# Block 1 of a two-block transformer kernel: modulation sums moved to the stage of keys and values, projections spread over all attention turns, convolution taps moved

## The chip, the cores and the metric

One core of a Trainium2 chip (trn2). The metric is the device time of one execution in microseconds (us), the median of several runs. Engines: PE multiplies matrices (PEld is its weight load), DVE is the vector engine, ACT the scalar engine, POOL GpSimd; SP's queue (SPq) issues the weight loads.

## The reference

Two transformer blocks over 512 tokens of width 1024. The first one, up to its mixture of experts, is what the change touches:

```
m = silu(c) @ w_mod + b_mod        # 6 x 1024 columns: shift, scale, gate, twice; also for the context rows
h, hc = modulate(rmsnorm(x), sh1, sc1), modulate(rmsnorm(ctx), sh1c, sc1c)
proj = h @ w_in                    # q, k, v (512 each), glu (1024), gate_att (1024), gate_conv (1024)
att = neighbourhood_attention(q, k, v, k_ctx, v_ctx, rpb)      # 8 heads; 512 local + 256 context keys
u = a * sigmoid(g)                 # a, g: the halves of glu
y = silu(layernorm(conv(u, conv_w) + conv_b))                  # depthwise, 31 taps, 512 channels
x = x + g1 * ((sigmoid(gate_att) * (att @ w_ao) + sigmoid(gate_conv) * (y @ w_co)) @ w_o)
```

After it come a mixture of 32 experts, a second attention block and an expert layer with product keys. None of that code changes.

## The kernel before, in words

`do_b1` runs four stages. Activations lie transposed: 1024 channels as 8 tiles of 128 partitions, 512 tokens in the free dimension. A float32 product is made of three matmuls (`mm3`, lines 327 to 329) of a high part H, cast by ACT (line 180), and a low part L = x - H, made by DVE or POOL (line 189). One output tile of 128 channels, a projection, is 8 x 3 matmuls.

**Loads.** `Loader` keeps a ring of five 1 MB tiles (`ringA`) and loads the units in the order in which `b1_plan` lists them; a unit leaves when the oldest has been freed (line 116, on SP's queue, which goes in order). Kinds: ("in", m) is a column tile m of w_in, two (or, for the values, two row halves) to a unit; ("m1", 0 to 7) are modulation units multiplied on PE (`mod_unit`); ("m1", 8 to 23) are rows of w_mod's transpose (`w_modr`), for which `mod_rows` makes two DVE instructions with a running sum (line 594, 128x1024 times the row `crow`, which is silu(c) spread over all partitions). `Splitter` makes H and L ahead of use, two pieces ahead in block 1.

**Stage 1, `project1`.** Norms, modulation of the latent and context rows, queries; then `keys`: four column tiles (m = 4 to 7) for latent and context rows (the cast of tile 5 stands on ACT behind the last copy of the queries, line 745), then `value_steps` over units 4 and 5. The activation Silu of `crow` stands in the values (lines 763 and 764, with a table load before and after).

**Stage 2, `attention1`.** 16 turns, four head pairs by four blocks of 128 queries. In a turn: the next turn's score products (line 862), its minimum on DVE (`least`, lines 875 to 880), this turn's transposes on PE (912) and copies on ACT (317), the next turn's exponents on ACT (888, 889), the product with the values (921, into a spare piece of the score tile), the copy of its result, and the next turn's scaling (896, 897 on DVE, 899 on ACT). Between these `Fill` puts PE's projections in steps of three matmuls: `fill1`, eight glu tiles over turns 0 to 7, one each; `fill2`, four tiles of gate_att over turns 8 to 15, half of one each. After each of the first eight turns stand `mod_rows` of one or two units (`early`). `glu_end` makes u for two channel tiles, with a table switch on ACT, when four glu tiles are there, and for the other two from turn 8. From then on `conv` puts convolution taps on DVE (`conv_steps`, line 782 the first of a channel tile, 786 the 30 others; the running sum is `g`, in SBUF): a credit of 2.4 ahead of the product with the values and of 2.4 behind the scaling, at 0.66 a tap.

**Stage 3, `merge`.** Twelve more gate projections (m = 4 to 15), with up to nine taps after each; at m = 12 the convolution is finished and PE's sums for the layernorm over it follow (line 241). Then the output products.

Of the kernel before, what the change touches and what calls it, by code (L numbers as in the profile page):

```python
# [285 lines left out]
class Kern:  # L286
# [231 lines left out]
                else:  # L518
                    sp.add_rows(key, 16 if s[0] == "d" else 2, 2, half)

    @staticmethod
    def early(n):

        return (2 * n, 2 * n + 1) if n < 5 else (n + 5,)

    def b1_plan(self):

        plan = [("m1", 0), ("m1", 4)] + [("in", m) for m in range(4)]
        for u in range(1, 4):
            plan += [("m1", u), ("m1", 4 + u)]  # L530
        plan += [("in", m) for m in range(4, 12)]
        self.fill1 = []
        for m, i in enumerate((0, 1, 4, 5, 2, 3, 6, 7)):
            self.fill1 += [("in", 12 + i)]
            plan += [("in", 12 + i)] + [("m1", 8 + j) for j in self.early(m)]
        plan += [("in", 20 + m) for m in range(16)]
        for n in ("ao", "co", "wo"):
            for m in range(8):
                plan.append((n, m))
                if n == "wo":  # L540
                    plan.append(("m2", m))
                elif n == "ao" and m in (1, 3, 5):
                    plan.append(("m1", 21 + m // 2))
        return plan
# [36 lines left out]
            nc.tensor.matmul(pm[:, h, :], sb[:, h * 128:(h + 1) * 128], self.c("msel"), start=True, stop=True)  # L581
        nc.scalar.copy(self.mod1[:, 2 * u:2 * u + 2, :], pm)

    def mod_row(self, pool, i):

        self.crow = pool.tile([128, D], F32, name="crow")
        self.nc.gpsimd.dma_start(out=self.crow, in_=self.ap["crow"][:, i * D:(i + 1) * D])

    def mod_rows(self, which, u):
# [52 lines left out]
    def do_b1(self):  # L642
        nc, tc, ap = self.nc, self.tc, self.ap
        V = nc.vector
        with ExitStack() as es:
            hp = es.enter_context(tc.tile_pool(name="h", bufs=1))
            sm = es.enter_context(tc.tile_pool(name="sm", bufs=1))
            self.sp.ahead = 2
            self.sp.low = "g"
            self.sp.use(es.enter_context(tc.tile_pool(name="w", bufs=1)))  # L650
            cv = es.enter_context(tc.tile_pool(name="cv", bufs=1))
            hH = hp.tile([128, KD, T], F32R, name="hH", tag="hH")
            hL = hp.tile([128, KD, T], F32R, name="hL", tag="hL")
            h = (hH, hL)
            x = self.xT
            self.mod_row(sm, 0)
            qT = cv.tile([128, 4, T], F32, name="qT", tag="qT")
            with ExitStack() as e2:
                kv = e2.enter_context(tc.tile_pool(name="kv", bufs=1))
                kT = kv.tile([128, 4, T + CTX], F32, name="kT")  # L660
                v = kv.tile([128, 6, 512], F32, name="v")
                with tc.tile_pool(name="ps1", bufs=1, space=PSUM) as ps, tc.tile_pool(name="w0", bufs=1) as w0:
                    self.mod_start(w0)
                    nc.scalar.preload_act_table_set("natural_log_exp_and_others")
                    self.project1(cv, w0, ps, sm, x, h, qT, kT, v)
                u_t = cv.tile([128, 4, T + 30], F32, name="u", tag="u")
                g_t = cv.tile([128, 4, T], F32, name="g", tag="g")
                gA = cv.tile([128, 4, T], F32, name="gA", tag="gA")
                nc.gpsimd.memset(u_t[:, :, 0:15], 0.0)
                nc.gpsimd.memset(u_t[:, :, 15 + T:], 0.0)  # L670
                conv = Fill([self.conv_steps(u_t, g_t)], 124 * 0.66)
                self.attention1(h, qT, kT, v, u_t, g_t, gA, conv, sm)
            self.merge(hp, cv, h, g_t, qT, gA, conv, sm)
        self.sp.ahead = 1
        self.sp.pool = None

    def project1(self, hcp, extra, ps, sm, x, h, qT, kT, v):
# [24 lines left out]
        for u in range(4):  # L702
# [3 lines left out]
                self.mod_unit("m1", 4 + u, ps, extra)  # L706
            if u == 0:
                nc.sync.dma_start(out=cx, in_=ap["ctx"])
            else:
                part(2 * u - 2, (2, 3))  # L710
            self.mod_flush(ps)
# [35 lines left out]
        def keys(w, m, lat):  # L747
            pt = ps.tile([128, T], F32, name="pt", tag="fl", bufs=4)[:, :T if lat else CTX]
            for k in range(KD):
                g = h if lat else hc  # L750
                self.mm3(pt, (w[0][:, k], w[1][:, k]), (g[0][:, k], g[1][:, k]), k == 0, k == KD - 1)
            nc.scalar.copy(kT[:, m - 4, 0 if lat else T:T if lat else T + CTX], pt)
        w = [self.sp.get(("in", 2)), self.sp.get(("in", 2), False)]
        for lat in (True, False):
            for i in range(2):
                keys(w[i], 4 + i, lat)
        for m in (6, 7):
            w = self.sp.get(("in", 3))
            for lat in (True, False):
                keys(w, m, lat)  # L760
        for n, _ in enumerate(self.value_steps(("in", 4), ps, h, v, hc, (("fl", 4, 1),))):
            if n == 2:
                nc.scalar.activation(self.crow, self.crow, AF.Silu)
                nc.scalar.preload_act_table_set("natural_log_exp_and_others")
            if n in (8, 30):
                self.load_bias((8, 30).index(n) * 2, 2)
        self.sp.low = "g"
# [9 lines left out]
    def conv_steps(self, u_t, y):  # L777
# [1 line left out]
        V = self.nc.vector  # L779
        cw = self.p("conv_w").rearrange("p (k t) -> p k t", k=4)  # L780
        for k in range(4):
            V.tensor_scalar(y[:, k], u_t[:, k, 0:T], cw[:, k, 0:1], self.p("conv_b")[:, k:k + 1],
                            op0=OP.mult, op1=OP.add)
            yield 0.66
            for t in range(1, 31):
                V.scalar_tensor_tensor(y[:, k], u_t[:, k, t:t + T], cw[:, k, t:t + 1], y[:, k],
                                       op0=OP.mult, op1=OP.add)
                yield 0.66

# [38 lines left out]
    def attention1(self, h, qT, kT, v, u_t, g_t, gA, conv, sm):  # L828
# [3 lines left out]
        with tc.tile_pool(name="a1", bufs=1) as a1, tc.tile_pool(name="ps2", bufs=1, space=PSUM) as ps:  # L832
# [16 lines left out]
            def gate(m):  # L849
                return self.dmaj_steps(("in", 10 + m // 2), h, ps, lambda pt: nc.scalar.copy(gA[:, m], pt))  # L850

            fill1 = Fill([glu(i - 12) for n, i in self.fill1], 8 * 5.3)
            fill2 = Fill([gate(m) for m in range(4)], 4 * 5.3)
            spare = [None]

            def products(hp, i):
# [73 lines left out]
            for n, (hp, i) in enumerate(seq):  # L930
# [5 lines left out]
                        self.load_bias(2 * seq[n + 1][0] + 4, 2)  # L936
                else:
                    spare[0] = ps.tile([128, CTX + 128], F32, name="cxs0", tag="cxs0")[:, CTX:]
                fill, left = (fill1, 8 - n) if n < 8 else (fill2, 16 - n)
                us = fill.left / left  # L940
                PTs = turn(Ps, fill)
                if nxt:
                    Ps = exps(cxs, Pm)
                fill.run(0.5 * us - 0.7)
                if n > first:
                    conv.run(2.4)
                if (n >= 8 or first > n) and len(glus) >= 4 * (1 + (n >= 8)) and ends:
                    first = min(first, n)
                    glu_end(ends.pop(0))
                pv(hp, i, PTs)  # L950
                if nxt:
                    scaled(Ps)
                fill.run(0.5 * us)
                if left == 1:
                    fill.finish()
                if n < 8:
                    for j in self.early(n):
                        self.mod_rows("m1", 8 + j)
                if n > first:
                    conv.run(2.4)  # L960

# [38 lines left out]
    def merge(self, hp, cv, h, y, att, gA4, conv, sm):  # L1000
        nc, tc, ap = self.nc, self.tc, self.ap
        V = nc.vector
        with tc.tile_pool(name="mg", bufs=1) as mg, tc.tile_pool(name="ps3", bufs=1, space=PSUM) as ps:
# [9 lines left out]
                nc.scalar.activation(gA4[:, m], gA4[:, m], AF.Sigmoid)  # L1013
            na = 0
            norm = self.layernorm(cv, ps, sm, y)
            for m in range(4, 16):
                i = 20 + m
                g = gA(m) if m < 8 else gB[:, m - 8]
# [1555 lines left out]
```

## Time and profile before

| | us |
|---|---|
| median of three runs | 2775.05 (2774.60 to 2776.61) |
| the profiled execution | 2774.60, its span 2772.8 |
| attention, first score product to last gate projection | 141.88 to 336.12 |
| PE, DVE, ACT, POOL busy over the span | 2595.9, 1793.1, 1038.7, 640.7 |
| mean granted clock of PE | 0.972 |

Block 1 takes about the first 500 us of the span. In rows of the trace, a time in square brackets is how long the engine stood idle before the instruction, and behind it is what ended that. [...]

### The profile page before, as it was taken

The page shows a single profiled execution, that of the slowest core. Times are in us where ns is not written, and L with a number is a line of the kernel's source. Part 1 is how long each engine was busy: PE and PEld are TensorE (multiplying, and loading weights), DVE is VectorE, ACT ScalarE, POOL GpSimd, SP SyncE. Part 2 cuts the span into 40 slices and gives each one's busy share as a digit, 9 for nine tenths or more (in the row PEclk, how much of TensorE's full clock was granted, in tenths as well). Part 3 has the DMA queues.
Part 4 walks back from the last instruction along what each step waited for, and adds up shares of the span by engine and source line. Part 5 has one row for each costly group of instructions (what it writes and reads, how often), then busy time and mean ns, then how long its engine had stood idle before and what let it go on. Part 6 is the DMA issues. An engine that isn't in the chain of part 4 may idle for free.

```text
span 2772.8 us, 36809 instructions
## 1 busy us (share of the span) xinstructions
PE 2595.9 (94%) x13993; PEld 2015.7 (73%) x13993; DVE 1793.1 (65%) x3214; ACT 1038.7 (37%) x1930; POOL 640.7 (23%) x430
## 2 busy tenths in 40 slices
PE   7977889899999998999899998999999999999998
PEld 4855567654454444768779988999999988888886
DVE  4258977632323334654628999878774777888887
ACT  3256624311111113243533332577773333333333
POOL 1122144300000001000323333333332443222232
PEclk9989999899989999999999999999999999999999
DMA  7243123779979994531034555688887779999994
GB/s 309 75 158 142 62 76 137 280 314 416 419 314 418 416 420 187 215 135 62 16 106 168 202 170 207 207 284 306 320 299 278 286 281 341 359 350 349 350 364 171
DMA packets 190100, 691.11 MB, mean 249 GB/s; under 512 B 16608, under 2 KB 92000, under 8 KB 135264
## 3 DMA queue, kind: packets, MB, share of 16 engines
q1 hardware_dynamic: 151696, 546.10, 52.4%
q0 software_dynamic: 37936, 139.48, 14.3%
q10 hardware_dynamic: 288, 3.15, 0.3%
q8 instruction: 111, 1.82, 0.3%
q14 instruction: 69, 0.57, 0.1%
HBM read 639.24 MB, written 49.41 MB: 248 GB/s over the span
## 4 chain that ended last, share of the span: by engine, by line
PE 44%; DVE 13%; ACT 3%; issue 2%; POOL 0%; DMA 0%; DVEq 0%; ACTq 0%; POOLq 0%; SPq 0%
PE acc L327 6%; PE acc L329 6%; PE acc L328 6%; PE pS L327 4%; PE pS L329 4%; PE pS L328 4%; PE pg L2130 3%; DVE rows L2321 2%; DVE wL L189 1%; PE pt L327 1%; PE pt L329 1%; PE pt L328 1%; PE gu L1354 1%; DVE oo L2110 1%; PE Y L1381 1%
## 5 line engine op out<-in xcount | busy, mean ns | idle before, releaser
L189 DVE TENSOR_TENSOR wL<-ringA,wH 128x1024 fp32r<-128x1024 f32 x277 | 339.5, 1231 | 184.3 <-ACT wH L180 180.9
L180 ACT CAST wH<-ringA 128x1024 fp32r<-128x1024 f32 (+1 forms) x359 | 367.0, 1027 | 69.0 <-PE acc L329 20.8
L189 POOL TENSOR_TENSOR wL<-ringA,wH 128x1024 fp32r<-128x1024 f32 (+1 forms) x82 | 191.8, 2343 | 869.1 <-ACT wH L180 855.7
L329 PE MATMUL pS<-hH,wL 128*128 128x384 f32 x1024 | 347.2, 339 | 13.8 <-DVE wL L189 13.8
L327 PE MATMUL pS<-hH,wH 128*128 128x384 f32 x1024 | 355.7, 347 | 0.6 <-ACT gS L1954 0.6
L328 PE MATMUL pS<-hL,wH 128*128 128x384 f32 x1024 | 346.4, 338 | 0.0
L329 PE MATMUL acc<-wH,AL 128*128 128x512 f32 x768 | 304.9, 397 | 2.5 <-DVE AL L2230 2.5
L327 PE MATMUL acc<-wH,AH 128*128 128x512 f32 x768 | 305.0, 397 | 1.6 <-ACT AH L2226 1.6
L2302 POOL DMA_INDIRECT rows<-e_dn,idx x128 | 202.3, 1580 | 447.1 <-DVE rows L2321 413.8
L328 PE MATMUL acc<-wL,AH 128*128 128x512 f32 x768 | 304.7, 397 | 0.0
L2302 POOL DMA_INDIRECT rows<-e_up,idx x128 | 149.1, 1165 | 333.1 <-DVE ht L2345 312.2
L327 PE MATMUL pt<-hH,wH 128*128 128x512 f32 x512 | 217.4, 425 | 7.8 <-ACT hH L393 4.9
L328 PE MATMUL pt<-hL,wH 128*128 128x512 f32 x512 | 208.1, 406 | 2.5 <-DVE hL L379 2.5
L329 PE MATMUL pt<-hH,wL 128*128 128x512 f32 x512 | 207.6, 405 | 2.1 <-DVE wL L189 2.1
L329 PEld LDWEIGHTS pS<-hH,wL 128*128 128x128 f32 x1024 | 194.0, 189 | 15.4 <-DVE wL L189 15.4
L327 PEld LDWEIGHTS pS<-hH,wH 128*128 128x128 f32 x1024 | 194.6, 190 | 2.7 <-ACT gS L1954 0.9
L328 PEld LDWEIGHTS pS<-hL,wH 128*128 128x128 f32 x1024 | 194.5, 190 | 1.7
L2226 ACT CAST AH<-A 128x384 fp32r<-128x384 f32 x128 | 65.8, 514 | 300.9 <-PE acc L328 243.5
L329 PEld LDWEIGHTS acc<-wH,AL 128*128 128x128 f32 x768 | 144.9, 189 | 38.7 <-DVE AL L2230 3.7
L327 PEld LDWEIGHTS acc<-wH,AH 128*128 128x128 f32 x768 | 144.8, 189 | 35.5 <-ACT AH L2226 1.9
L328 PEld LDWEIGHTS acc<-wL,AH 128*128 128x128 f32 x768 | 144.8, 189 | 33.8
L2345 DVE SCALAR_TENSOR_TENSOR ht<-rows,S,ht 128x1024 f32<-128x1024 f32 x127 | 162.6, 1280 | 2.7 <-DMA rows<-e_up,idx 2.0
(503 smaller groups left out, 4979.9 us busy)
## 6 DMA issues: line engine op xcount, KB each, us to landing
ringA<-t_dn SPq DMA_DIRECT2D x64, 1024.0 KB, 6.6
ringA<-t_up SPq DMA_DIRECT2D x64, 1024.0 KB, 7.6
ringB<-w_eu SPq DMA_DIRECT2D x42, 1024.0 KB, 13.1
ringA<-w_ed SPq DMA_DIRECT2D x39, 1024.0 KB, 9.3
ringB<-w_eg SPq DMA_DIRECT2D x37, 1024.0 KB, 13.5
ringA<-w_in SPq DMA_DIRECT2D x30, 1024.0 KB, 5.1
ringA<-w_eg SPq DMA_DIRECT2D x28, 1024.0 KB, 11.0
ringB<-w_ed SPq DMA_DIRECT2D x27, 1024.0 KB, 8.7
```

What stands on the lines that cost most here:

```text
L180: self.kern.nc.scalar.copy(H, v)
L189: (self.kern.nc.vector if self.low == "v" else self.kern.nc.gpsimd).tensor_tensor(out=L, in0=v, in1=H, op=OP.subtract)
L327: te.matmul(ps, a[0], b[0], start=start, stop=False, skip_group_check=skip)
L328: te.matmul(ps, a[0], b[1], start=False, stop=False, skip_group_check=skip)
L329: te.matmul(ps, a[1], b[0], start=False, stop=stop, skip_group_check=skip)
L1354: nc.tensor.matmul(gu[m][64 * s:64 * s + 64], xg[:, 4 * u + k, o:o + 64], w[s][:, k], start=u == 0 and k == 0, stop=u == 1 and k == 3, ski ...
L1381: nc.tensor.matmul(Y[64 * s:64 * s + 64], aT[:, k, 64 * s:64 * s + 64], w[s][:, k, lo:hi], start=k == 0, stop=k == 3, skip_group_check=True)
L2130: nc.tensor.matmul(pg[:, t], o2[:, t], o1[:, t], start=True, stop=True)
L2226: nc.scalar.copy(AH, A)
L2302: k.nc.gpsimd.indirect_dma_start(out=self.rows[:, p % self.R], out_offset=None, in_=k.ap[src], in_offset=bass.IndirectOffsetOnAxis(ap=self ...
L2321: nc.vector.scalar_tensor_tensor(u, u, 1.0, self.ht, op0=OP.mult, op1=OP.mult, accum_out=self.S[:, n - 3:n - 2])
L2345: V.scalar_tensor_tensor(self.ht, u, self.S[:, p:p + 1], self.ht, op0=OP.mult, op1=OP.add)
```

## The change

- `b1_plan`: the units ("m1", 8 to 20) no longer stand between the glu units, but between the units of keys and values; all units of w_in from 12 on follow in one go. `early` is gone.
- `project1`: `crow` is loaded behind the first modulation step, its Silu stands ahead of the keys, and `mod_rows` of units 8 to 15 between the key tiles, of 16 to 20 in the values.
- `attention1`: one `fill` of twelve projections over all 16 turns; the taps' credit ahead of the product with the values is 1.2 instead of 2.4; `glu_end` goes by the number of glu tiles alone.
- `conv_steps`: channel tiles that begin in the merge have their running sum in PSUM (`cy`, two tiles); the last tap writes `g`.

```diff
     def b1_plan(self):
...
-        plan += [("in", m) for m in range(4, 12)]
-        self.fill1 = []
-        for m, i in enumerate((0, 1, 4, 5, 2, 3, 6, 7)):
-            self.fill1 += [("in", 12 + i)]
-            plan += [("in", 12 + i)] + [("m1", 8 + j) for j in self.early(m)]
-        plan += [("in", 20 + m) for m in range(16)]
+        plan += [("in", m) for m in range(4, 8)] + [("m1", m) for m in range(8, 12)]
+        plan += [("in", 8), ("in", 9)] + [("m1", m) for m in range(12, 16)]
+        plan += [("in", 10), ("in", 11)] + [("m1", m) for m in range(16, 21)]
+        self.fill = (0, 1, 4, 5, 2, 3, 6, 7, 8, 9, 10, 11)
+        plan += [("in", 12 + i) for i in self.fill] + [("in", 24 + m) for m in range(12)]
...
+        nc.scalar.activation(self.crow, self.crow, AF.Silu)
+        nc.scalar.preload_act_table_set("natural_log_exp_and_others")
         w = [self.sp.get(("in", 2)), self.sp.get(("in", 2), False)]
         for lat in (True, False):
             for i in range(2):
                 keys(w[i], 4 + i, lat)
+                self.mod_rows("m1", 8 + 2 * (not lat) + i)
         for m in (6, 7):
             w = self.sp.get(("in", 3))
             for lat in (True, False):
                 keys(w, m, lat)
+                self.mod_rows("m1", 2 * m + (not lat))
         for n, _ in enumerate(self.value_steps(("in", 4), ps, h, v, hc, (("fl", 4, 1),))):
-            if n == 2:
-                nc.scalar.activation(self.crow, self.crow, AF.Silu)
-                nc.scalar.preload_act_table_set("natural_log_exp_and_others")
+            if n % 9 == 4 and n < 41:
+                self.mod_rows("m1", 16 + n // 9)
...
         for k in range(4):
-            V.tensor_scalar(y[:, k], u_t[:, k, 0:T], cw[:, k, 0:1], self.p("conv_b")[:, k:k + 1],
+            a = self.conv_ps.tile([128, T], F32, name="cy", tag="cy", bufs=2) if self.conv_ps else y[:, k]
+            V.tensor_scalar(a, u_t[:, k, 0:T], cw[:, k, 0:1], self.p("conv_b")[:, k:k + 1],
                             op0=OP.mult, op1=OP.add)
             yield 0.66
             for t in range(1, 31):
-                V.scalar_tensor_tensor(y[:, k], u_t[:, k, t:t + T], cw[:, k, t:t + 1], y[:, k],
+                V.scalar_tensor_tensor(y[:, k] if t == 30 else a, u_t[:, k, t:t + T], cw[:, k, t:t + 1], a,
                                        op0=OP.mult, op1=OP.add)
...
-            fill1 = Fill([glu(i - 12) for n, i in self.fill1], 8 * 5.3)
-            fill2 = Fill([gate(m) for m in range(4)], 4 * 5.3)
+            fill = Fill([glu(m) if m < 8 else gate(m - 8) for m in self.fill], 12 * 5.3)
...
-                fill, left = (fill1, 8 - n) if n < 8 else (fill2, 16 - n)
-                us = fill.left / left
+                us = fill.left / (16 - n)
...
                 if n > first:
-                    conv.run(2.4)
-                if (n >= 8 or first > n) and len(glus) >= 4 * (1 + (n >= 8)) and ends:
+                    conv.run(1.2)
+                if len(glus) >= 12 - 4 * len(ends) and ends:
...
-                if left == 1:
+                if n == 15:
                     fill.finish()
-                if n < 8:
-                    for j in self.early(n):
-                        self.mod_rows("m1", 8 + j)
...
             norm = self.layernorm(cv, ps, sm, y)
+            self.conv_ps = ps
```

The instruction order shows three places. First ACT from the last copy of the queries (qT) through the keys (kT); wH is the high part of a weight piece. Before:

```order
L745 ACTIVATE qT<-pt 128x512
L180 CAST wH<-ringA 128x1024 x2
L752 COPY kT<-pt 128x512 x2
L752 COPY kT<-pt 128x256 x2
L180 CAST wH<-ringA 128x1024 x2
```

Now:

```order
L745 ACTIVATE qT<-pt 128x512
L753 ACT_TABLE_LOAD
L753 ACTIVATE crow<-crow 128x1024
L754 ACT_TABLE_LOAD
L180 CAST wH<-ringA 128x1024 x2
L752 COPY kT<-pt 128x512 x2
L752 COPY kT<-pt 128x256 x2
L180 CAST wH<-ringA 128x1024 x2
```

Two table loads and the Silu now stand ahead of the casts of key tiles 5 and 6.

Second SP's queue, the weight loads from key tile 4 to the end of the gates (w_in), with the modulation units (w_modr) between them. Before:

```order
L116 DMA ringA<-w_in 128x2048 x5
L116 DMA ringA<-w_modr 128x2048 x4
L116 DMA ringA<-w_in 128x2048
L116 DMA ringA<-w_modr 128x2048 x4
L116 DMA ringA<-w_in 128x2048
L116 DMA ringA<-w_modr 128x2048 x3
L116 DMA ringA<-w_in 128x2048
L116 DMA ringA<-w_modr 128x2048 x2
L116 DMA ringA<-w_in 128x2048 x8
```

Now:

```order
L116 DMA ringA<-w_in 128x2048 x2
L116 DMA ringA<-w_modr 128x2048 x4
L116 DMA ringA<-w_in 128x2048
L116 DMA ringA<-w_modr 128x2048 x4
L116 DMA ringA<-w_in 128x2048
L116 DMA ringA<-w_modr 128x2048 x5
L116 DMA ringA<-w_in 128x2048 x12
```

The 13 modulation units have moved ahead of the glu units; units 4 and 5 of w_in (the values) now have four of them in front.

Third DVE behind the last scaling of the attention (s is a row sum, g and cy the running sum of the convolution, u its input). Before:

```order
L897 RECIPROCAL s_2581<-s_2581 128x1
L786 SCALAR_TENSOR_TENSOR g<-u,prm,g 128x512 x23
L782 TENSOR_SCALAR g<-u,prm 128x512
L786 SCALAR_TENSOR_TENSOR g<-u,prm,g 128x512 x30
L980 TENSOR_TENSOR g<-g,bc 128x512 x2
```

Now:

```order
L900 RECIPROCAL s_2539<-s_2539 128x1
L790 SCALAR_TENSOR_TENSOR g<-u,prm,g 128x512 x16
L786 TENSOR_SCALAR cy<-u,prm 128x512
L790 SCALAR_TENSOR_TENSOR cy<-u,prm,cy 128x512 x29
L790 SCALAR_TENSOR_TENSOR g<-u,prm,cy 128x512
L786 TENSOR_SCALAR cy<-u,prm 128x512
L790 SCALAR_TENSOR_TENSOR cy<-u,prm,cy 128x512 x29
L790 SCALAR_TENSOR_TENSOR g<-u,prm,cy 128x512
L979 TENSOR_TENSOR g<-g,bc 128x512 x2
```

Where 54 taps stood, 78 stand; 16 of them in SBUF, 62 with the sum in PSUM.

## Rows read from the trace of the kernel before

**Rows 1.** The page, its 40 equal slices: PE's granted clock in tenths.
```profile
PEclk9989999899989999999999999999999999999999
```

**Rows 2.** Busy time by stretch: us, PE, PEld, DVE, ACT, POOL, clock, DMA share, GB/s.
```profile
141.88:336.12 194.24, 153.13 (x992) 110.34 (x992) 153.50 (x335) 120.03 (x264) 42.78 (x21) 0.92 0.33 118
148.00:168.00 20.00, 11.80 (x65) 9.39 (x66) 5.59 (x16) 9.02 (x19) 4.75 (x2) 0.74 0.15 53
```

**Rows 3.** Who waited for whom, PE, 68 to 420 us: total, times, longest.
```profile
PE cxs L921 <- ACT P L889: 38.4, 15, 8.2
```

**Rows 4.** Order of time, 158 to 256 us: start, us, engine, line, operation, tiles, form.
```profile
158.01 1.04 ACT L180 CAST wH<-ringA 128x1024 fp32r<-128x1024 f32 x1 [7.70 <-DMA ringA<-w_in]
...
161.03 2.83 PE L921 MATMUL cxs<-PT,v 128*64 128x128 f32 x24 [8.20 <-ACT P L889]
...
164.70 1.21 DVE L594 SCALAR_TENSOR_TENSOR ringA<-ringA,crow 128x1024 f32<-128x1024 f32 x1
...
167.09 10.42 SPq L116 DMA_DIRECT2D ringA<-w_modr  x4
...
187.80 2.83 PE L921 MATMUL cxs<-PT,v 128*64 128x128 f32 x24 [4.16 <-ACT P L889]
...
243.68 3.28 DVE L594 SCALAR_TENSOR_TENSOR ringA<-ringA,crow 128x1024 f32<-128x1024 f32 x1
...
255.88 2.83 PE L921 MATMUL cxs<-PT,v 128*64 128x128 f32 x24 [6.74 <-ACT P L889]
```

**Rows 5.** Order of time, turns of the attention on PE.
```profile
147.82 0.87 PE L912 MATMUL t<-cst,P 128*128 128x128 f32 x6
...
206.39 1.13 PE L862 MATMUL loc<-kT,qT 64*128 64x512 f32 x4
...
212.01 1.53 PE L921 MATMUL cxs<-PT,v 128*64 128x128 f32 x24 [0.50 <-ACT P L889]
...
216.46 1.13 PE L862 MATMUL loc<-kT,qT 64*128 64x512 f32 x4
...
272.30 1.13 PE L862 MATMUL loc<-kT,qT 64*128 64x512 f32 x4
...
321.20 1.13 PE L862 MATMUL loc<-kT,qT 64*128 64x512 f32 x4
```

**Rows 6.** Order of time, keys and values: PE, DVE, the Silu of crow on ACT.
```profile
75.74 0.50 PE L327 MATMUL pt<-hH,wH 128*128 128x512 f32 x1 [1.18 <-ACT wH L180]
...
91.02 2.36 DVE L189 TENSOR_TENSOR wL<-ringA,wH 128x1024 fp32r<-128x1024 f32 x2 [11.03 <-ACT wH L180]
...
107.85 0.28 PE L328 MATMUL pvv<-wL,hH 128*128 128x256 f32 x1
...
107.85 1.28 ACT L763 ACT_TABLE_LOAD   x1
109.15 1.06 ACT L763 ACTIVATE crow<-crow 128x1024 f32<-128x1024 f32 x1
110.22 1.28 ACT L764 ACT_TABLE_LOAD   x1
```

**Rows 7.** Order of time, taps on DVE, and PE's sums for the layernorm.
```profile
274.25 3.09 DVE L786 SCALAR_TENSOR_TENSOR g<-u,prm,g 128x512 f32<-128x512 f32 x4
...
329.19 25.98 DVE L786 SCALAR_TENSOR_TENSOR g<-u,prm,g 128x512 f32<-128x512 f32 x23
...
393.34 1.92 PE L241 MATMUL cs<-g,one 128*32 128x512 f32 x2 [8.61 <-DVE g L786]
```

**Rows 8.** DVE's groups, 330 to 520 us: busy, mean ns, idle before them.
```profile
L1046 DVE TENSOR_TENSOR gB<-gB,gA 128x512 f32<-128x512 f32 x8 | 9.7, 1210 | 0.3
...
L1057 DVE SCALAR_TENSOR_TENSOR xT<-pt,mod,xT 128x512 f32<-128x512 f32 x8 | 6.0, 751 | 18.4 <-PE pt L329 18.4
...
L1045 DVE TENSOR_TENSOR gB<-pt,gB 128x512 f32<-128x512 f32 x8 | 5.5, 685 | 2.5 <-PE pt L329 2.5
```

**Rows 9.** DMA issues, 60 to 260 us: KB each, median us to landing.
```profile
ringA<-w_modr SPq DMA_DIRECT2D x13, 1024.0 KB, 4.8
```

More of the change, by code (lines that the diff above doesn't have):

```diff
@@ L519, in plan @@
                     sp.add_rows(key, 16 if s[0] == "d" else 2, 2, half)
-    @staticmethod
-    def early(n):
-        return (2 * n, 2 * n + 1) if n < 5 else (n + 5,)
     def b1_plan(self):
@@ L582, in mod_flush, with mod_row, mod_load @@
         nc.scalar.copy(self.mod1[:, 2 * u:2 * u + 2, :], pm)
-    def mod_row(self, pool, i):
+    def mod_row(self, pool, i, load=True):
         self.crow = pool.tile([128, D], F32, name="crow")
+        if load:
+            self.mod_load(i)
+    def mod_load(self, i):
         self.nc.gpsimd.dma_start(out=self.crow, in_=self.ap["crow"][:, i * D:(i + 1) * D])
@@ L655, in do_b1 @@
             x = self.xT
-            self.mod_row(sm, 0)
             qT = cv.tile([128, 4, T], F32, name="qT", tag="qT")
@@ L664, in do_b1 @@
                     nc.scalar.preload_act_table_set("natural_log_exp_and_others")
+                    self.mod_row(sm, 0, False)
                     self.project1(cv, w0, ps, sm, x, h, qT, kT, v)
@@ L671, in do_b1 @@
                 conv = Fill([self.conv_steps(u_t, g_t)], 124 * 0.66)
+                self.conv_ps = None
                 self.attention1(h, qT, kT, v, u_t, g_t, gA, conv, sm)
@@ L708, in project1 @@
                 nc.sync.dma_start(out=cx, in_=ap["ctx"])
+                self.mod_load(0)
             else:
```

## The prediction

> **What bounds the kernel now.** I read the page first, then the stretches, then waits, then the order of time. The change touches block 1 alone, the first 480 us of the span, so I looked for what ends last there. The granted clock dips in three places of the page's slices of 69 us [rows 1]: in the first, in the third and fourth (the attention), and in the sixth.
>
> In the stretches [rows 2] the attention (from the first score product at 141.88 to the last gate projection at 336.12) lasts 194.2 us, with PE busy 153.1 and DVE 153.5: neither is full, so in the attention PE waits. In the merge the one long wait is that of the layernorm's sums for DVE, 8.61 us [rows 7].
>
> The waits say for what PE waits in the attention [rows 3]: the product with the values (line 921) waits 38.4 us in 15 places for ACT's exponents, which are in front of it because it writes into a spare piece of their score tile. In order of time [rows 4] the exponents are late for two reasons. Twice ACT stands at a weight cast for a DMA (7.70 us; PE then idles 8.20 and, in the third turn, 4.16): the w_in unit sits behind modulation units in SP's queue. Later DVE is the late one: a modulation sum of 3.28 us (1.21 undisturbed) and another behind it stand ahead of the next turn's minimum, and PE idles 6.74. [...]
>
> **The change, part by part.**
>
> *Attention: projections spread, sums gone.* A quiet turn is the one from 206.39 to 216.46: 10.07 us with one whole projection (24 matmuls) in it [rows 5]. Its product with the values starts 5.62 us after its score product (212.01), after 0.50 of waiting for ACT. With three quarters of a projection, PE's own work there is shorter by a quarter of 24 matmuls at 0.24 us (12 of them stand between 213.54, where the product ends, and 216.46), 1.4 us: 8.67. That is the floor of a turn. But the 5.62 is a chain over DVE's minimum and ACT's exponents that less filling does not shorten. So I take 5.62, the product 1.53, and half of the filling, nine matmuls at 0.24 or 2.18: 9.33. The ceiling is a turn of the second half, where DVE is full of taps: five turns between 272.30 and 321.20 give 9.78 with half a projection [rows 5], so 11.2 with three quarters. I take 9.33, near the quiet row, since DVE now has no sums, nothing at all before the seventh turn, then two taps ahead of the scaling for four. 16 turns: 149.3.
>
> To that come: the start, 5.94 us from the first score product to the first turned probabilities (147.82) instead of the quiet turn's 1.5 [rows 5], 4.4; less 2 in the last turn, which has no next products; four turns in which copy and cast of a projection now stand between ACT's copies of the turned probabilities and delay the exponents, 1.04 for the cast [rows 4] and an estimated 0.6 for the copy, the first with two casts, 7; the two switches of ACT's tables for the sigmoid gates, two loads of 1.28 each as in [rows 6], estimated at 2.5 each since PE has filling to go on with, 5; taps that still hold up a scaling, 2. Together 149.3 + 4.4 - 2 + 7 + 5 + 2 = 165.7 against 194.2: **28.5 us won**. The DMA waits go, since SP now issues all twelve w_in units in a row and each lasts two projections, 18 us, against 4.8 us for landing a unit [rows 9].
>
> *The Silu of the row c moves.* Before, two table loads and the activation ran in the stage of values, 3.65 us on ACT (107.85 to 111.50) with PE busy meanwhile [rows 6]. Now they stand ahead of the cast that key tile 5 needs. PE already waits 1.18 us for that cast at 75.74 [rows 6]; so all 3.65 is added, and PE's gap is 4.8 us. After the gap of 4.16 us the product took 2.83 instead of 1.53 and five matmuls some 0.2 more each [rows 4, 5], 2.3 us; I take 2.5. **6.1 lost**, between 3.7 (no dip) and 9. What is late next, the lows of the second key unit, shifts with it. [...]
>
> *The sums in the stage of keys and values.* 26 sums at 1.21 [rows 4] (two in a unit) are 32 us on a DVE that is nearly idle there, on no path by themselves. They wait for 13 w_modr units. Behind them on DVE stand the lows of w_in units 4 and 5, PE waits for those, and SP's queue puts unit 5 behind four of those loads. The chain: the last low of unit 3, over at 92.2 before [rows 6], comes 6.1 later, at 98.3, and frees unit 3; unit 4 and four w_modr leave. Unit 4 lands at 103.1, its first low is made at 105.4; if the others land 2.5 us apart, two of them take four sums, to 110.6, and the second low of unit 4 is there at 111.8. PE first wants it at 107.85 + 6.1 = 114.0 [rows 6]. Price nothing; its cover is those 2 us, and without it see the second rival.
>
> *Taps.* In the attention the change leaves 46 taps where there were 70, so 78 follow instead of 54. Before, the tail ran from 329.19 to 393.28, 64.1 us, 1.13 for each of the first 23 taps and by the remainder 1.23 for the other 31 [rows 7], and PE, which came to the mean's matmuls at 384.7, idled 8.61. Undisturbed, four taps take 3.09 [rows 7], 0.78 pitch; the rest is POOL's splits. Of the 78, 16 still run in SBUF, 18 us. The last 62 have their running sum in PSUM. No row shows DVE writing PSUM. The nearest: in the merge, with POOL at work, sums of two SBUF tiles take 1210 ns but those with one operand in PSUM 685, and a scalar-tensor-tensor with a PSUM operand 751 [rows 8]. So 0.78: 48 us, tail 65.5. PE comes later too: turn 15's last quarter and the merge's eight and a quarter projections are 57.8 after that point (55.5 before). It idles 7.7: **0.9 won**. Bounds: 0.70 a tap wins 5 more; 1.23, the contended rest, costs 28. [...]
>
> *Sum:* -28.5 + 6.1 - 0.9 = -23.3 against the profiled execution's own 2774.6 (the median of the runs is 2775.05): **2751 us**. What follows block 1 depends on its end alone, the expert loads too, so I let the gain through.
>
> **Rivals.**
> 1. *The turns stay long*: the chain over ACT and DVE, not PE's filling, sets them, as in the second half. For it: five such turns took 9.78 each with half a projection, 2.9 us less of PE's work than the quiet turn has, yet only 0.3 less time [rows 5]. 16 x 11.2 + 4.4 is 184: won 10, net -5, or half way -14: 2770 to 2761. Against: those turns carry eight taps, the new ones two plus four.
> 2. *The lows come late behind the sums.* If the w_modr units land one by one at their median of 4.8 us [rows 9] instead of 2.5, the second low of unit 5, behind seven of them, is made some 15 us late, and unit 6 some 7 more: 2751 + 22 = 2773, no change. Against: four such units left within 10.42 us [rows 4], so they overlapped, and at 2.5 us apart the chain above holds.
> 3. *Slower: taps in PSUM are dearer.* DVE's tail ends last in the merge already, so every ns counts from the first. From 1.24 us a tap, 28.5 over 62 taps, the kernel is slower by more than 0.2%. If PSUM does not free a tap from POOL, with the factor of 1210 to 685 it takes 1.38: 37 us, 2788. Against: rows 8.
> 4. *Better*: turns at the floor of 8.67 (10 us) and no dip in the keys: 2740.
>
> **Chances.** Forecast, 2742 to 2760: 0.64. Long turns 0.12, half of it within the bound; late lows 0.10, the most within; slower 0.06; better 0.08. The range leaves out the slower case, the worst of rivals 1 and 2 and the last of 4: 2738 to 2769. What a measurement can tell from no change is 0.2%, 5.5 us. Faster 0.84, same 0.09, slower 0.07.
>
> **What would show it.** Right: no ACT wait for w_in in the attention, turns of 9 to 9.8 us, the attention at 160 to 172 us, its clock near 1; a PE gap near 4.8 us at 75; lows of units 4 and 5 with no PE wait; PSUM taps near 0.75 to 0.8 and a wait of 5 to 10 us before the mean. Wrong: PE waits for wL in the values, turns above 10, taps in PSUM above 1 us.

## The result, and the profile after

The changed kernel takes 2749.77 us in the median of four runs (2746.03 to 2754.29), beside 2774.85 for the kernel before, also in four runs; the ratio is 0.9909, 95% interval 0.9898 to 0.9921. The forecast was 2751. The profiled execution took 2749.65, with a span of 2747.9, 24.9 less than before.

Where the time went, by stage, from the order of time on PE: the start of the first key product, of the first score product, of the first projection of the merge and of the last product of the mean.

| from, to | before | after | difference | forecast |
|---|---|---|---|---|
| start to first key product | 68.72 | 67.29 | -1.4 | 0 |
| keys and values | 73.16 | 79.13 | +6.0 | +6.1 |
| attention | 194.88 | 168.52 | -26.4 | -28.5 |
| merge to the mean's last product | 56.58 | 53.22 | -3.4 | -0.9 |
| sum | 393.34 | 368.16 | -25.2 | -23.3 |

From there on all rows stand 25 us earlier, to the end. The page's slices show the granted clock of the kernel after, in tenths of full speed:

```profile
PEclk9999999899999999999999999999999999999999
```

The 8 in the third slice of [rows 1], which holds the first third of the attention, is gone. The prediction put the dips of before in the wrong slices: they stand in the third, the eighth and the twelfth, and only the third lies in what the change touches. (The twelfth reads 9 now, but the same work, at 763 to 832 us before and 738 to 807 after, has a clock of 0.88 in both; only the edges of the slices moved.)

Busy time by stretch (PE, PEld, DVE, ACT, POOL, clock, DMA share, GB/s), kernel after: the attention up to its last gate projection, its start, and the stage of keys and values; the last row is that stage before.

```profile
146.42:314.30 167.88, 147.42 (x992) 104.89 (x992) 104.49 (x260) 118.47 (x264) 43.06 (x21) 0.98 0.17 56
148.00:168.00 20.00, 18.72 (x93) 13.08 (x94) 8.21 (x33) 13.63 (x31) 4.71 (x2) 0.83 0.16 54
67.29:146.42 79.13, 71.99 (x480) 65.70 (x480) 46.73 (x69) 19.97 (x28) 9.72 (x8) 0.94 0.64 234
```

```profile
68.72:141.88 73.16, 70.39 (x480) 64.67 (x480) 17.76 (x17) 19.86 (x28) 11.00 (x8) 0.98 0.21 72
```

Against [rows 2] DVE lost 49 us of work in the attention, the idle time of PE fell from 41 to 20, and the clock rose from 0.92 to 0.98. PE's own busy time is 5.7 us shorter for the same 992 matmuls, at the higher clock. The waits of PE say the same (kernel after; the first row against [rows 3]; the last two are those of the keys and values):

```profile
PE cxs L924 <- ACT P L892: 14.7, 15, 1.3
...
PE pt L327 <- ACT wH L180: 4.9, 1, 4.9
...
PE pvv L328 <- DVE wL L189: 0.4, 1, 0.4
```

15 waits for the exponents are still there, but the longest is 1.3 us, not 8.2. ACT's two waits for a load of w_in in the attention are gone; before they were

```profile
ACT wH L180 <- DMA ringA<-w_in: 11.1, 2, 7.7
```

The place where the change loses, in order of time (kernel after; before, the product at 75.74 of [rows 6] answers to the one at 78.05):

```profile
73.30 1.28 ACT L753 ACT_TABLE_LOAD   x1
74.60 1.06 ACT L753 ACTIVATE crow<-crow 128x1024 f32<-128x1024 f32 x1
...
75.66 1.28 ACT L754 ACT_TABLE_LOAD   x1
76.95 1.99 ACT L180 CAST wH<-ringA 128x1024 fp32r<-128x1024 f32 x2
78.03 3.50 DVE L189 TENSOR_TENSOR wL<-ringA,wH 128x1024 fp32r<-128x1024 f32 x2 [4.69 <-ACT wH L180]
78.05 0.79 PE L327 MATMUL pt<-hH,wH 128*128 128x512 f32 x1 [4.92 <-ACT wH L180]
...
80.44 0.79 PE L329 MATMUL pt<-hH,wL 128*128 128x512 f32 x1 [1.17 <-DVE wL L189]
```

The casts wait behind the Silu, PE for the cast 4.92 us and then 1.17 for the second low; a matmul behind the gap takes 0.79 where it took 0.50. Further on, DVE's lows of w_in, and the taps and the mean (kernel after, order of time, against [rows 6, 7]):

```profile
95.58 2.36 DVE L189 TENSOR_TENSOR wL<-ringA,wH 128x1024 fp32r<-128x1024 f32 x2 [4.89 <-ACT wH L180]
104.00 1.23 DVE L189 TENSOR_TENSOR wL<-ringA,wH 128x1024 fp32r<-128x1024 f32 x1 [1.47 <-ACT wH L180]
...
304.61 14.56 DVE L790 SCALAR_TENSOR_TENSOR g<-u,prm,g 128x512 f32<-128x512 f32 x16
319.09 0.81 DVE L786 TENSOR_SCALAR cy<-u,prm 128x512 f32<-128x512 f32 x1
319.94 22.92 DVE L790 SCALAR_TENSOR_TENSOR cy<-u,prm,cy 128x512 f32<-128x512 f32 x29
...
368.16 1.92 PE L241 MATMUL cs<-g,one 128*32 128x512 f32 x2 [5.25 <-DVE g L790]
```

29 taps with their sum in PSUM take 22.92 us, 0.79 each, while POOL, which splits weights, is busy for 16.5 of them; the second 29 take 22.92 as well, with POOL busy for 9.6. PE waits 5.25 for the mean, not 8.61.

### The profile page after: what moved, and what is told of

It reads as the page before. It is cut to its first block, busy times and chain, and to the rows that moved or that the text cites. A ratio compares the mean times of both kernels' runs of the same rounds, so it can differ in the third digit from the quotient of the medians.

```text
span 2747.9 us, 36821 instructions
## 1 busy us (share of the span) xinstructions
PE 2593.2 (94%) x13993; PEld 2011.3 (73%) x13993; DVE 1771.1 (64%) x3214; ACT 1036.9 (38%) x1930; POOL 635.8 (23%) x430
## 4 chain that ended last, share of the span: by engine, by line
PE 44%; DVE 13%; ACT 4%; issue 2%; DMA 1%; POOL 0%; DVEq 0%; ACTq 0%; POOLq 0%; SPq 0%
PE acc L327 6%; PE acc L329 6%; PE acc L328 6%; PE pS L327 4%; PE pS L329 4%; PE pS L328 4%; PE pg L2130 2%; DVE rows L2321 2%; DVE wL L189 2%; PE pt L327 1%; PE pt L329 1%; PE pt L328 1%; DVE oo L2110 1%; PE gu L1354 1%; ACT wH L180 1%
## 6 DMA issues: line engine op xcount, KB each, us to landing
ringA<-w_eg SPq DMA_DIRECT2D x28, 1024.0 KB, 11.2
```

## The experiments

The theory: the modulation sums on DVE and the loads between the w_in units held up ACT's exponents, and their going is the 26 us; the Silu ahead of the casts costs about 6; PSUM keeps the last taps out of POOL's way. Rivals: the spread of the projections makes the gain, or the loads alone; PSUM does nothing; the gap at 78 us is not the Silu's. All kernels below compute the whole result. Their ratios are to the kernel before, and stage lengths come from their profiled executions. Four kernels with the same attention (the changed one, the late Silu, the taps in SBUF, the early load of c) took 165.7 to 168.5 us for it, so 3 us there is what one profile can't tell apart. Of these 3 us, 2.0 stand in the first turn and what is ahead of it: 17.09 us from 146.42 at a granted clock of 0.80 in the changed kernel's profile, 15.11 at 1.00 in the other three. Behind that the four lie within 1.4 us.

**The Silu behind the casts.**

```
+        w = [self.sp.get(("in", 2)), self.sp.get(("in", 2), False)]
         nc.scalar.activation(self.crow, self.crow, AF.Silu)
         nc.scalar.preload_act_table_set("natural_log_exp_and_others")
-        w = [self.sp.get(("in", 2)), self.sp.get(("in", 2), False)]
```

> The changed kernel with one thing moved: the Silu of the row c and the table load behind it now come after the cast of the second half of the first key unit, not ahead of it. Theory (the 4.9 us for which PE waits in front of key tile 5, and the lower clock behind them, are the price of the 3.65 us that the two table loads and the activation take on ACT): the gap falls to about the 1.2 us that it had in the kernel before, and with the dip that goes with it the run is 4 to 6 us shorter, 2744 to 2746. [...]

Measured: 2742.69, ratio 0.9879 (0.9864 to 0.9894), clear of the changed kernel's interval. Busy time by stretch of this kernel, keys and values, then attention:

```profile
68.19:141.47 73.28, 70.37 (x481) 64.65 (x481) 49.54 (x69) 19.97 (x28) 10.86 (x8) 0.98 0.68 253
141.47:307.18 165.71, 145.84 (x993) 103.93 (x993) 102.64 (x261) 118.81 (x266) 42.77 (x21) 0.99 0.17 59
```

PE's waits for the cast and for the second low are back to what they were before:

```profile
PE pt L327 <- ACT wH L180: 1.3, 1, 1.3
...
PE pt L329 <- DVE wL L189: 0.5, 1, 0.5
```

The keys and values are 73.28 us with all 26 sums in them, 5.85 less than in the changed kernel and as long as before without sums. The gap is the Silu's; the sums are free there. Of the 7 us between the medians 5.85 are this stage's, the rest is inside the scatter of the attention.

**Taps in SBUF again.**

```
-            self.conv_ps = ps
```

> The changed kernel with the running sums of the last taps in SBUF again, everything else as changed. Theory (a tap in SBUF is held up by POOL's splits in the merge, 1.13 to 1.23 us as in the kernel before, and one with its sum in PSUM is not, 0.79): 62 taps times 0.34 to 0.44 is 21 to 27 us, all of it ahead of the layernorm's mean, for which PE waits already: 2771 to 2777, so that the gain of the change is gone. Rival (with the taps behind the scaling, POOL is no hindrance: the 16 taps that run in SBUF at the start of this tail took 0.91 us each): 62 times 0.12 is 7 us, 2757. Second rival (nothing): 2750.

Measured: 2770.08, ratio 0.9982 (0.9974 to 0.9991): 20 us of the 25 are gone. Its last taps and PE's mean, in order of time:

```profile
317.83 45.67 DVE L790 SCALAR_TENSOR_TENSOR g<-u,prm,g 128x512 f32<-128x512 f32 x30
...
364.00 23.59 DVE L790 SCALAR_TENSOR_TENSOR g<-u,prm,g 128x512 f32<-128x512 f32 x30
...
387.65 1.91 PE L241 MATMUL cs<-g,one 128*32 128x512 f32 x2 [23.04 <-DVE g L790]
```

The first 30 taps take 1.52 us each, beside POOL, which is busy for 31 of those 46 us; the second 30, when POOL is done, 0.79. POOL pays too: its nine splits there take 2.71 us each, beside taps in PSUM 2.40. So it is not an even 1.2: a tap in SBUF costs twice as much while POOL works, 1.52 us, and the same as one in PSUM when it doesn't, 0.79. The changed kernel's 29 taps with their sum in PSUM took 22.92 us whether POOL was busy beside them for 16.5 us or for 9.6.

**The projections divided as before**, one in each of the first eight turns, half a one in each of the last.

```
-            fill = Fill([glu(m) if m < 8 else gate(m - 8) for m in self.fill], 12 * 5.3)
+            fill1 = Fill([glu(m) for m in self.fill[:8]], 8 * 5.3)
+            fill2 = Fill([gate(m - 8) for m in self.fill[8:]], 4 * 5.3)
...
```

> The changed kernel with the projections of the attention divided as before: one whole projection in each of the first eight turns, half a one in each of the last eight. The sums stay in the stage of keys and values and the loads in the changed order. Theory A (the prediction's arithmetic: a turn with three quarters is 9.33 us, against 10.07 with a whole and 9.78 with half a projection): the attention is 16 times 0.6 us, 9.5, longer: 2759. Theory B (the spread wins nothing; what counted was that ACT and DVE no longer stand at loads and sums: the changed kernel's turns measured 10.24 us, no less than the mean of 10.07 and 9.78): the attention within 4 us of its 167.9, and since the first four gated projections are ready some turns sooner, some 15 to 20 more taps run inside the attention, the tail is that much shorter and PE's wait of 5.25 us for the mean goes: 2743 to 2750.

Measured: 2747.65, ratio 0.9905 (0.9890 to 0.9920), the same as the changed kernel. The attention is 168.21 us against 168.52. Theory B: the spread by itself wins nothing. The tail is 3.5 us shorter in the profile, as expected, but the medians don't show it.

**The sums back in the attention**, two at the end of each of 13 turns, with their units behind the w_in units.

```
-                self.mod_rows("m1", 8 + 2 * (not lat) + i)
...
+                if n < 13:
+                    self.mod_rows("m1", 8 + n)
```

> The changed kernel with the modulation sums back in the attention, two a turn at the end of the first 13 turns, three of their units behind each w_in unit in the order of the loads; the projections stay spread. Theory (a sum on DVE stands ahead of the next turn's minimum and so ahead of ACT's exponents): two sums are 2.4 us undisturbed; half of that or more in each of 13 turns is not hidden, the attention 15 to 30 us longer, 2765 to 2780, with PE's waits for ACT's exponents back above 25 us. Rival (DVE has room, 104 of 168 us busy; the waits of the kernel before came from the order of the loads alone): the attention within 4 us, 2746 to 2754. In both the stage of keys and values is as long as with the sums, within 1 us.

Measured: 2766.97, ratio 0.9972 (0.9961 to 0.9982). The attention is 185.41 us, 16.9 longer, though ACT waits for no load in it; the keys and values 78.88 against 79.13. The dearest turn of this kernel, in order of time:

```profile
224.95 5.62 POOL L775 TENSOR_TENSOR bias<-bias,cst 128x896 f32<-128x896 f32 x2 [3.88 <-DMA bias<-rpbx]
...
226.00 10.61 DVE L788 SCALAR_TENSOR_TENSOR g<-u,prm,g 128x512 f32<-128x512 f32 x4
...
236.53 0.68 DVE L876 CUSTOM_DVE_ANT_0 P<-loc,bias 128x512 f32<-128x512 f32 x1
...
237.84 0.72 ACT L889 ACTIVATE P<-P,m 128x512 f32<-128x512 f32 x1 [7.65 <-DVE m L881]
...
239.16 2.83 PE L922 MATMUL cxs<-PT,v 128*64 128x128 f32 x24 [8.95 <-ACT P L890]
```

The sums shift the taps to where POOL adds the bias and splits; four taps then take 10.61 us, not 3.09, the minimum behind them is late, then ACT, then PE. So a sum costs its own time and moves other DVE work into POOL's way.

**Sums back, and four taps ahead of the product with the values** (two after the change). Three differences from the attention before are left: the order of the loads, the division, and the turns in which the sums stand (a unit in each of 13 turns; before, two or one in each of the first eight).

```
-                    conv.run(1.2)
+                    conv.run(2.4)
```

> The changed kernel with the modulation sums back in the attention (as in the run of that kind) and, on top, four taps ahead of the product with the values, not two, as before the change. What is then left of the difference from the attention before, 194.9 us, is the order of the loads (the equal division of the projections moved the attention by 0.3 us only). Theory A (the loads: the two DMA waits of before cost PE 8.20 and 4.16 us): the taps do little, attention 183 to 187 us against 185.4 with two taps ahead. Theory B (the taps ahead of the scaling, which cost 4.6 us with the sums gone, cost more with them there): attention 190 to 195 us, and the order of the loads is worth 5 or less.

Measured: 2773.92, ratio 1.0003 (0.9993 to 1.0013); the attention 190.32 us. The two taps are 4.9 us, and 4.6 are left to 194.88, as theory B had it. But those 4.6 are not the price of the loads, since the sums stand in other turns. That price can be read turn by turn, from score product to score product, against the run with the projections divided as before, whose turns hold the same projections:

| turn | before | sums gone, division as before | what stands in it before |
|---|---|---|---|
| first | 23.86 | 13.75 | ACT's wait of 7.70 for a load; no sum has run yet |
| third | 16.96 | 10.90 | ACT's wait of 3.42 for a load |
| seventh | 15.35 | 11.60 | sums, taps, POOL's bias |
| eighth | 18.92 | 11.45 | sums, taps, POOL's splits |

The other turns differ by 1.3 us or less. So of the 26.7 us between these two attentions the turns with the two load waits hold 16.2 and those where sums meet taps and POOL 11.2. Loads alone, as a rival, are out: neither run with the sums back has such a wait, and their attentions are still 17 and 22 us longer than the changed one. But the loads are the larger part of what the change won, which the 4.6 hides.

**Four taps ahead, with the late Silu.** The edit is that of the late Silu and the `conv.run(2.4)` above.

> The version with the late Silu, and the number of taps ahead of the product with the values as before: four a turn, not two, with four behind the scaling as changed. Theory (taps ahead of the scaling hold it up, and the scaling is in front of the next turn's transposes): about nine turns, two taps of 0.78 us more in each, half to all of it on the path, 7 to 14 us; PE's wait of 5.0 us for the mean and then 0 to 5 us more of DVE's tail are won, since 18 fewer taps follow; 2743 to 2752. Rival (DVE has 60 us of room in the attention and those taps cost nothing): the wait for the mean goes, 2738.

Measured: 2747.08, ratio 0.9899 (0.9884 to 0.9914). The attention is 170.31, 4.6 longer than with the late Silu alone, but 2.0 of this stand ahead of the first tap (17.08 us there at a clock of 0.80, against 15.11 at 1.00). The taps are left with 2.6, far less than expected and little more than the scatter. The tail won nothing, for a reason that neither theory had: with more taps in the attention the third of the four channel tiles began there, so its sum went to SBUF, and 30 of its taps took 39.51 us. The edit doubles one cost to save another, and the expected 5 us of shorter tail never came.

**All taps behind the scaling, with the late Silu.**

```
-                if n > first:
-                    conv.run(1.2)
...
-                    conv.run(2.4)
+                    conv.run(3.6)
```

> The version with the late Silu, and all taps of a turn behind the scaling: none ahead of the product with the values, six behind it. The number in the attention is the same, so the tail is too. Theory (the two taps ahead still hold up the scaling by up to 1.5 us in some nine turns): the attention 5 to 10 us shorter than 165.7, 2733 to 2738. Rival (six taps in a row, 4.7 us, reach into the next turn's minimum, and ACT's exponents come later by what the scaling wins): within 3 us of 2742.7, or slower.

Measured: 2753.04, ratio 0.9922 (0.9908 to 0.9935): the theory fell, the rival held. The attention is 174.43. In order of time, the first turn with taps:

```profile
216.33 2.12 POOL L777 TENSOR_TENSOR bias<-bias,cst 128x896 f32<-128x896 f32 x1 [0.33 <-DMA bias<-rpbx]
...
216.49 1.98 DVE L899 TENSOR_TENSOR s<-s 128x1 f32<-128x1 f32 x1
...
219.15 5.90 DVE L790 SCALAR_TENSOR_TENSOR g<-u,prm,g 128x512 f32<-128x512 f32 x5
...
227.60 2.83 PE L924 MATMUL cxs<-PT,v 128*64 128x128 f32 x24 [4.37 <-ACT P L892]
```

Six taps in a row (the first is another instruction, not in these rows) reach into the next minimum, PE waits 4.37 us and the product behind the gap takes 2.83, not 1.53.

**The load of the row c at the start again.**

```
+            self.mod_row(sm, 0)
...
-                self.mod_load(0)
```

> The changed kernel with one thing undone: the load of the row c, 0.5 MB, leaves on POOL's queue at the start of the program again, beside the slices of x. Theory (the later load lets the slices of x land sooner; the first key product stood at 67.29 us in the changed kernel and at 68.72 before): the first key product back at 68.7, all else the same, 2751. Rival (the start varies by as much from run to run: with the later load it stood at 67.3, 67.3, 68.2, 68.3 and 68.9 in five profiles): anywhere in 67 to 69 and the time as the changed kernel's, 2750 give or take 3.

Measured: 2748.15, ratio 0.9905 (0.9890 to 0.9920), no difference. The first key product stood at 69.16; in the other profiles with the late load it stood between 67.3 and 69.4. The 1.4 us of the table's first row are not shown to be the change's.

**The late Silu with the division as before.** Both edits are above.

> The version with the late Silu, and the projections divided as before: a whole one in each of the first eight turns, half a one in each of the last eight. Theory (each of the two alone was measured: the late Silu 0.0030 of the time below the changed kernel, the division as before no different from it in the attention, 168.2 against 168.5 us, but with 3.5 us less of tail): the gains add, 2739 to 2741, PE's wait for the mean near 1.5 us. Rival (the division before wins nothing in any median): 2743.

Measured: 2740.23, ratio 0.9884 (0.9869 to 0.9899), not to be told from the late Silu alone. PE's wait for the mean fell to 2.06 us.

**More of the filling ahead of the product with the values** (late Silu). PE's 15 waits of some 1 us for the exponents are most of what is left of the attention's waits.

```
-                fill.run(0.5 * us - 0.7)
+                fill.run(0.65 * us - 0.7)
...
-                fill.run(0.5 * us)
+                fill.run(0.35 * us)
```

> The version with the late Silu, and in each turn more of the filling ahead of the product with the values: 0.65 of it, not half. The work is the same. Theory (what is left of the waits in the attention is PE at the product with the values, 14.9 us in 15 places, while ACT's exponents are made; matmuls moved there from behind the product fill it, and the scaling behind the product ends about 1 us before the transposes that want it): the attention 5 to 9 us shorter than 165.7, 2734 to 2738. Rival (the turn is a cycle over ACT and DVE, and what is filled at one place is waited for at the next, at the transposes): PE's waits for the scaling instead, 2740 to 2745.

Measured: 2737.88, ratio 0.9866 (0.9848 to 0.9885), which overlaps with the late Silu alone; but the attention is 160.64 us and PE's wait for the exponents 8.7.

> The same with 0.8 of the filling ahead of the product. Theory: the wait for the exponents, about 1 us a turn, is gone in all turns, and some 0.3 us of waiting for the scaling comes in its place; the attention 8 to 12 us shorter than 165.7, 2731 to 2735. Rival (a cycle over ACT and DVE): 2740 to 2745, with PE's waits at the transposes of 8 us or more.

Measured: 2733.07, ratio 0.9845 (0.9831 to 0.9860), below the interval of the late Silu alone; the attention 156.67 in a profile that is the slowest of its five runs. Its waits of PE in the attention:

```profile
PE cxs L865 <- ACT qT L317: 2.3, 1, 2.3
PE cxs L865 <- DVE qT L315: 2.1, 1, 2.1
PE t L915 <- ACT P L902: 1.8, 3, 1.0
PE cxs L924 <- ACT P L892: 1.5, 2, 1.0
```

and two of its turns on PE in order of time:

```profile
157.07 1.13 PE L865 MATMUL loc<-kT,qT 64*128 64x512 f32 x4
...
162.80 1.53 PE L924 MATMUL cxs<-PT,v 128*64 128x128 f32 x24
...
165.15 1.13 PE L865 MATMUL loc<-kT,qT 64*128 64x512 f32 x4
...
174.63 1.13 PE L865 MATMUL loc<-kT,qT 64*128 64x512 f32 x4
```

The wait for the exponents went from 14.9 us (late Silu alone) to 1.5, and at the transposes PE waits 1.8 for the scaling, not the 8 of the rival: down to this length the turn is no cycle over ACT and DVE. From score product to product with the values it is 5.73 us, as long as the chain of 5.62 in [rows 5], but with no wait in it.

> The version with 0.8 of the filling ahead of the product and the late Silu, and the projections divided as before (a whole one in each of the first eight turns, half a one in each of the last eight). Theory (filling placed where PE waits, and the shorter tail that this division gave, 3.5 us): 2728 to 2733. Rival (in the last eight turns half a projection is too little to fill both places): the attention as long as with the equal division at half, 2738 to 2742.

Measured: 2726.64, ratio 0.9829 (0.9812 to 0.9846), the fastest here, by the medians 23 us below the changed kernel. Its stretches, in a profile that is the fastest of its five runs: keys and values, attention, merge to the mean.

```profile
68.31:139.96 71.65, 68.83 (x481) 63.49 (x481) 49.55 (x69) 20.06 (x28) 10.91 (x8) 1.00 0.70 260
139.96:295.56 155.60, 143.58 (x992) 102.63 (x992) 104.80 (x265) 118.64 (x266) 41.66 (x21) 1.00 0.18 62
295.56:346.00 50.44, 48.34 (x208) 38.08 (x209) 47.82 (x64) 18.74 (x26) 26.62 (x13) 1.00 0.36 125
```

The clock is 1.00 in all three; in the attention PE idles 12 us, not 20. In this kernel the same sums, taps and projections are done as in the changed one. Half a projection in the last eight turns was enough, which the rival denied.

## Why the prediction was right

*Attention, -28.5 forecast, -26.4 measured.* The reading of the waits held: no load in front of ACT, no wait for the exponents above 1.3 us, the clock at 0.98; and its two reasons, loads first and sums later, are the two pairs of turns in the table above, 16.2 and 11.2 us. Put back a unit a turn, the sums by themselves cost 17; two taps ahead of the scaling cost 4.9 with the sums there and 2.6 without. But the part was headed "projections spread, sums gone", and the spread wins nothing: attention 168.21 without it, where the arithmetic of the turn asks for 9.5 more. So the 28.5 was met in part by luck. What the step got wrong is the turn. It took 9.33 bare and 16.4 us of extras beside the turns, 10.4 in all; the turns came out at this kernel's rows:

```profile
163.51 1.13 PE L865 MATMUL loc<-kT,qT 64*128 64x512 f32 x4
172.17 1.13 PE L865 MATMUL loc<-kT,qT 64*128 64x512 f32 x4
182.93 1.13 PE L865 MATMUL loc<-kT,qT 64*128 64x512 f32 x4
...
214.26 1.13 PE L865 MATMUL loc<-kT,qT 64*128 64x512 f32 x4
...
225.83 1.13 PE L865 MATMUL loc<-kT,qT 64*128 64x512 f32 x4
...
296.63 1.13 PE L865 MATMUL loc<-kT,qT 64*128 64x512 f32 x4
```

13 turns from 163.51 to 296.63 are 10.24 on the mean, from 8.66 (the floor of 8.67 was met once, in the first of them) to 11.57 (from 214.26, with the first sigmoid gates between). So the prediction's own mark for right, "turns of 9 to 9.8", failed, and its mark for wrong, "turns above 10", came true, while the sum held to 2.1 us: the marks were set for a bare turn, but in the trace the extras lie inside the turns. Turn for turn 10.24 lies midway between the bare 9.33 and the first rival's 11.2, but the rival's attention of 184 us did not come. "A chain over DVE's minimum and ACT's exponents that less filling does not shorten" was right and stopped short: the chain can be filled, and the run with 0.8 of the filling there has two turns in 17.56 us, 8.78 each.

*Silu, +6.1 forecast, +6.0 measured.* The gap of 4.8 was 4.92. The rest is not the dip alone: 1.17 at the second low, before 0.5, is a wait that the step left out, and PE's busy time rose by 1.6 where 2.5 was allowed for. These two misses nearly cancel, so the total is better than its parts. Of a switch the trace shows the load alone, 1.28: the activation starts 1.30 after the start of the first load, the cast 1.29 after that of the second. The 9 at which the step ended its range is shown by no run.

*Sums in the keys and values, price nothing.* Right by two runs: 78.88 without them against 79.13, and 73.28 with them when the Silu is out of the way. The chain behind it was too late: it had the second low of unit 4 ready at 111.8, with a cover of 2 us; it was there at 105.2 (the row at 104.00), and PE's wait of 0.4 is the one of before. The step that failed is "frees unit 3; unit 4 and four w_modr leave": unit 4 took the place that the first two sums had left, at 83.84 in SP's order of time, not behind the last low of unit 3.

```profile
83.84 0.33 SPq L116 DMA_DIRECT2D ringA<-w_in  x1
```


*Taps, -0.9 forecast, -3.4 measured.* The PSUM price of 0.78 was 0.79 (62 taps from 319.09 to 368.11, 49.0 us against 48). The mis-sized term is the 16 taps still in SBUF, 18 us forecast and 14.56 measured: 0.91 each, where the row of before had 1.13. The traces show why: beside the 23 taps of before (329.19 to 355.17) POOL ran five instructions, 11.8 us, and beside these 16 (304.61 to 319.09) one split of 2.95, since they end just before POOL's splits of the merge begin at 319.41. The third rival, dearer taps in PSUM, is out: 22.92 us for 29 is the pitch of 0.79 that the last 30 taps in SBUF had too (23.59).

*The load of the row c* had no term at all. Nothing came of it that a run could show.

## What to carry to other kernels

Price work on an engine that is far from full by what is queued behind it, not by the share of time: 26 sums on a DVE that was busy 105 of 168 us cost 17 us there and nothing one stage earlier. In a queue that goes in order, look also at what stands in front of a load that PE's work needs: the two turns with such a wait held 16 us. Ahead of an activation that needs another table, look which cast PE waits for next and put that first: 7 us here for one line moved. And before filling is spread evenly, find the one place in the turn where PE waits, and put the filling there: that won 10 to 14 us (2742.69 to 2733.07, 2740.23 to 2726.64) where the even spread won none.

## What the runs showed of the hardware

In these traces even a tiny DVE instruction with two inputs in SBUF stood until the POOL instruction beside it was over: with all taps behind the scaling, the 128x1 sum at 216.49 took 1.98 us, to 218.47, with a bias add of 2.12 on POOL from 216.33 to 218.45, and the like sum before it, at 216.23, took 0.15. In the changed kernel the 128x1 sums at 180.33, 182.35 and 224.19 took 1.90 to 1.97 us beside its bias adds; the reciprocal at 182.27, with one input, took 0.16 beside the same adds. That the running sum of a tap can stand in PSUM, be read and be written by the same DVE instruction at 0.79 us, and is then not held up by POOL's splits beside it (29 such taps in 22.92 us), no row of before had shown.
